# Inverse roots of a layer's RMS norms, spread over partitions by transposing their column instead of multiplying diagonal blocks by ones

## The chip, the cores and the metric

The kernel runs on one core of one Trainium2 chip. The core has five engines with queues of their own: TensorE (PE, matrix products; PEld is its weight load), VectorE (DVE), ScalarE (ACT), GpSimd (POOL) and SyncE (SP, which issues most DMA transfers). They work side by side and wait for each other by semaphores. The metric is the device time of one execution in microseconds (us), less being better.

## The reference

One decoder layer over 2048 tokens of width 1024, everything in float32: a norm, an input projection, two groups of heads side by side (a gated linear recurrence and attention with a sliding window), an output projection, a second norm, a gated feed-forward part with a short convolution, and a final norm. Cut to the norms and to where they stand:

```python
def rmsnorm(x, w, eps=EPS):
    inv = lax.rsqrt(jnp.mean(x * x, axis=-1, keepdims=True) + eps)
    return x * inv * w

u = rmsnorm(h, norm_mix_w)
proj = u @ w_in                      # 2048 x 1024 @ 1024 x 2816
...                                  # recurrence heads, attention heads -> mix
h = h + mix @ w_out
v = rmsnorm(h, norm_ffn_w)
gate = causal_depthwise_conv(v @ w_gate, conv_w, conv_b)
h = h + (silu(gate) * (v @ w_up)) @ w_down
return rmsnorm(h, final_norm_w)
```

A norm needs one number for each token: the inverse root of its mean square.

## The kernel before

**Layout.** Features lie on the 128 partitions and tokens along the free axis, eight tiles of 128 features for the width of 1024. The tokens go through in two halves of 1024 (the outermost loop). A norm's factor belongs to a token, that is to a column, and a column's factor must stand in all 128 partitions before an engine can multiply a tile by it. The kernel multiplies the matrix products first and applies the factor to their results, so a factor is needed only when a product is read back.

**Precision.** Each large product is made of three passes over split operands (high and low part); the names `XH` and `XL`, `whi` and `wlo` are these parts. Products inside the norms run on plain float32.

**A half.** The projections (names `kv`, `f`, `hq`, `q`, `g`, `pvv`, made by `unit`, line 195), the heads, the output projection (`pop`), then the feed-forward stage: eleven pairs of tiles through `pair_unit` (lines 674 to 676) for the gate and the up projection, and the down projection (`product`, lines 856 to 858), whose results `pdx` and `pdy` are added to the stream `h`. Behind the first half's down projection come the key and value projection `kv` and the first `f` of the second half.

**An inverse and its spread.** Class `Stats` holds a tile `acc` with the sums of squares, still apart for each partition. Its method `inverse` (lines 230 to 242) does three things. TensorE multiplies each block of 128 columns by a column of ones (line 236), which gives a column of totals, a token to a partition and a block to a column (`pst`). VectorE makes the inverse root of these few numbers by a bit trick and three Newton steps (`rsqrt`, lines 147 to 161, result `y`, the last step in line 160). Then VectorE writes diagonal blocks over `acc`: the identity times the column, a block of 128 columns for each (line 240). The method `spread` (lines 244 to 253) multiplies these blocks by a matrix of ones on TensorE (line 250, `pinv`, 512 columns at a time), so that each column's factor stands in every partition, and ScalarE copies the result back to `acc` (line 253).

**Where it happens.** Nine times: for the input norm `x` of each half (1024 columns, between the projections), for the feed-forward norm `h` of each half (1024 columns, inside the first `pair_unit`), for the final norm of the first half in two pieces of 512 columns (`o2` and `o`, among the `kv` projections of the second half, tile `sums`), and for the final norm of the second half in pieces of 512 (`o2`), 256 and 256 columns (`quarters`, `o`). The method `finish` (lines 944 to 948) multiplies the eight tiles of `h` by the factor and stores them. In the last two pieces it reads the factor from `pinv` itself, without a copy (`bank` given), and is bound by `issue_after(last)` to stand behind the last inverse.

**Order.** A scheduler orders the instructions of each engine by a simulated timeline of its own, within what the program's dependences and `issue_after` allow. An engine works through its own row in order.

Of the kernel before, what the change touches and what calls it, by code (L numbers as in the profile page):

```python
# [13 lines left out]
ALU = mybir.AluOpType  # L14
# [3 lines left out]
P = 128  # L18
D = 1024
# [26 lines left out]
def hymba_layer(ctx: ExitStack, tc: tile.TileContext, a: dict, out: bass.AP):  # L46
    nc = tc.nc

    def pool(name, bufs=1, space=None, stack=ctx, **kw):
        if space is not None:  # L50
            kw["space"] = space
        return stack.enter_context(tc.tile_pool(name=name, bufs=bufs, **kw))
# [12 lines left out]
    def ps(kind, name):  # L65
        return spaces[kind].tile([P, 512], F32, tag=kind, name=name)
# [9 lines left out]
    ones = cp.tile([P, P], F32, name="ones")  # L76
# [3 lines left out]
    ident = cp.tile([P, P], F32, name="ident")  # L80
# [63 lines left out]
        nc.vector.tensor_scalar(C.omlb, C.lb, -1.0, 1.0, op0=ALU.mult, op1=ALU.add)  # L144


    def rsqrt(ss, n, scale, keep=None):

        ms = sp.tile([P, n], F32, tag=f"ms{n}", name="ms")
        nc.vector.tensor_scalar(ms, ss, scale, EPS, op0=ALU.mult, op1=ALU.add)  # L150
        y = sp.tile([P, n], F32, tag=f"y{n}{keep}", name="y")
        yi = y.bitcast(I32)
        nc.vector.tensor_scalar(yi, ms.bitcast(I32), 1, None, op0=ALU.logical_shift_right)
        nc.vector.tensor_scalar(yi, yi, -1.0, float(0x5F3759DF), op0=ALU.mult, op1=ALU.add)
        nc.vector.tensor_scalar(ms, ms, -0.5, None, op0=ALU.mult)
        t = sp.tile([P, n], F32, tag=f"t{n}", name="t")
        for _ in range(3):
            nc.vector.tensor_tensor(t, y, y, op=ALU.mult)
            nc.vector.tensor_tensor(t, t, ms, op=ALU.mult)
            nc.vector.scalar_tensor_tensor(y, t, 1.5, y, op0=ALU.add, op1=ALU.mult)  # L160
        return y

    def raw4(src):
# [49 lines left out]
    class Stats:  # L213
# [16 lines left out]
        def inverse(self, keep):  # L230

            n = self.acc.shape[-1]
            nt = n // P
            st = ps("hg", "pst")
            for c in range(nt):
                nc.tensor.matmul(st[:, c:c + 1], self.acc[:, c * P:(c + 1) * P], ones[:, 0:1],
                                 start=True, stop=True)
            rs = self.rs = rsqrt(st[:, 0:nt], nt, 1.0 / D, keep)
            dg = self.acc
            return nc.vector.tensor_tensor(dg.rearrange("p (c t) -> p c t", t=P),  # L240
                                    ident.unsqueeze(1).to_broadcast([P, nt, P]),
                                    rs.unsqueeze(2).to_broadcast([P, nt, P]), op=ALU.mult)

        def spread(self, bank=None):

            n = self.acc.shape[-1]
            w = min(n, 512)
            for b in range(n // w):
                pb = ps(aux[b % 2 if bank is None else bank], "pinv")[:, 0:w]
                nc.tensor.matmul(pb, ones, self.acc[:, b * w:(b + 1) * w], start=True, stop=True)  # L250
                if bank is not None:
                    return pb
                nc.scalar.copy(self.acc[:, b * w:(b + 1) * w], pb)
# [150 lines left out]
    def hgrn(hf, h, X, invb, vs, WG, mix, p, fu=None):  # L404
# [100 lines left out]
        for c in range(TT):  # L505
# [4 lines left out]
            marks["po"] = nc.tensor.matmul(o, Q[:, cs], prev, start=False, stop=True)  # L510
            nc.scalar.activation(on[:, c], o, AF.Square, accum_out=ss[:, c:c + 1])
        rs = rsqrt(ss, TT, 1.0 / P)
        if h == HG - 1:
            mix[h] = new_x()
# [443 lines left out]
    for hf in range(NH):  # L958
        X, kv, invb, rs, f0 = nxt
        with ExitStack() as st:  # L960
            p = pool(f"mix{hf}", stack=st, reuse_waits="tile")
# [33 lines left out]
        with ExitStack() as st:  # L995
            p = pool(f"ffn{hf}", stack=st, reuse_waits="tile")
# [64 lines left out]
```

## Time and profile before

| | before |
|---|---|
| median of the runs | 2253.84 us (2253.62 to 2255.33, 3 runs) |
| span of the profiled execution (first to last instruction) | 2251.9 us |
| what lies between this span and the median | 1.9 us |
| mean granted TensorE clock | 0.990 |
| DMA, mean over the span | 113 GB/s |

The profiled execution has no device time of its own listed beside its span; the table sets the span against the median of the runs. The page gives the busy time of each engine and the chain of work that ended last; views of single lines give the duration of one instruction (least, median, most, in ns); the timeline gives start and length in us, merging neighbours of one kind (x4 is four instructions), and behind them in brackets the time its engine stood idle and what ended it. A matmul's record includes the time until its last result is out, so the records of neighbours overlap: what one costs in a stream is the distance between the ends of its neighbours, not its own length.

### The profile page before, as it was taken

The page shows a single profiled execution, that of the slowest core. Times are in us where ns is not written, and L with a number is a line of the kernel's source. Part 1 is how long each engine was busy: PE and PEld are TensorE (multiplying, and loading weights), DVE is VectorE, ACT ScalarE, POOL GpSimd, SP SyncE. Part 2 cuts the span into 40 slices and gives each one's busy share as a digit, 9 for nine tenths or more (in the row PEclk, how much of TensorE's full clock was granted, in tenths as well). Part 3 has the DMA queues.
Part 4 walks back from the last instruction along what each step waited for, and adds up shares of the span by engine and source line. Part 5 has one row for each costly group of instructions (what it writes and reads, how often), then busy time and mean ns, then how long its engine had stood idle before and what let it go on. Part 6 is the DMA issues. An engine that isn't in the chain of part 4 may idle for free.

```text
span 2251.9 us, 29785 instructions
## 1 busy us (share of the span) xinstructions
PE 2213.9 (98%) x11622; PEld 1862.1 (83%) x11622; DVE 1639.2 (73%) x2458; ACT 1024.6 (45%) x1781; POOL 7.2 (0%) x27
## 2 busy tenths in 40 slices
PE   8999999999999999999999999999999999999997
PEld 6988987778888888888889889887788888888887
DVE  6567467688888887885855665676888878887766
ACT  5345344454444444435724344435544444443353
POOL 1000000000000000000000000000000000000000
PEclk9999998999999999999999999989999999999999
DMA  4101002222323234974630101113232322359643
GB/s 151 38 29 38 29 29 75 94 85 84 118 88 122 89 122 134 360 254 148 207 122 29 38 29 29 53 51 121 67 114 97 115 92 98 107 179 390 225 136 127
DMA packets 89997, 254.19 MB, mean 113 GB/s; under 512 B 11008, under 2 KB 13184, under 8 KB 89856
## 3 DMA queue, kind: packets, MB, share of 16 engines
q1 hardware_dynamic: 87552, 251.17, 32.6%
q8 instruction: 91, 1.49, 0.3%
q10 hardware_dynamic: 2304, 1.12, 0.2%
q14 instruction: 50, 0.41, 0.1%
HBM read 195.10 MB, written 57.15 MB: 112 GB/s over the span
## 4 chain that ended last, share of the span: by engine, by line
PE 92%; DVE 4%; ACT 2%; DMA 2%; issue 1%; SPq 0%; DVEq 0%; ACTq 0%
PE X L674 7%; PE X L675 7%; PE X L676 7%; PE pop L195 6%; PE hq L195 4%; PE q L195 4%; PE f L195 4%; PE g L195 4%; PE Y L674 3%; PE Y L675 3%; PE Y L676 3%; PE pdx L856 3%; PE pdx L858 3%; PE pdx L857 3%; PE plev L454 3%; PE pdy L857 3%
## 5 line engine op out<-in xcount | busy, mean ns | idle before, releaser
L551 ACT CAST whi<-raw 128x1024 fp32r<-128x1024 f32 x88 | 92.6, 1053 | 118.6 <-PE X L675 72.8
L675 PE MATMUL X<-T,whi 128*128 128x512 f32 x352 | 137.8, 391 | 0.0
L674 PE MATMUL X<-T,whi 128*128 128x512 f32 x352 | 137.2, 390 | 0.0
L676 PE MATMUL X<-T,wlo 128*128 128x512 f32 x352 | 137.0, 389 | 0.0
L740 DVE SCALAR_TENSOR_TENSOR y<-ga,cw,y 128x1024 f32<-128x1024 f32 x88 | 112.6, 1280 | 25.4 <-ACT y L738 25.3
L176 ACT CAST whi<-raw 128x1024 fp32r<-128x1024 f32 (+2 forms) x61 | 63.0, 1036 | 123.8 <-PE q L195 59.1
L552 DVE TENSOR_TENSOR wlo<-raw,whi 128x1024 fp32r<-128x1024 f32 x88 | 107.3, 1219 | 0.0
L680 ACT COPY u<-X 128x512 f32<-128x512 f32 x88 | 51.6, 586 | 113.0 <-PE X L676 112.8
L552 DVE TENSOR_TENSOR xld<-raw,xhd 128x1024 fp32r<-128x1024 f32 x72 | 80.9, 1132 | 22.4 <-ACT xhd L551 22.0
L454 PEld LDWEIGHTS plev<-Q,K 128*128 128x128 f32 x640 | 82.8, 206 | 9.3 <-DVE K L463 4.5
L551 ACT CAST xhd<-raw 128x1024 fp32r<-128x1024 f32 x72 | 69.6, 978 | 45.9 <-DMA raw<-act0T 17.6
L454 PE MATMUL plev<-Q,K 128*128 128x64 f32 x640 | 83.5, 287 | 6.1 <-DVE K L463 6.1
L195 PE MATMUL pop<-XL,whi 128*128 128x512 f32 x256 | 84.5, 395 | 0.7 <-DVE XL L207 0.7
L195 PE MATMUL pop<-XH,wlo 128*128 128x512 f32 x256 | 84.4, 394 | 0.8 <-DVE wlo L177 0.8
L195 PE MATMUL pop<-XH,whi 128*128 128x512 f32 x256 | 84.3, 400 | 0.2
L462 DVE TENSOR_TENSOR Q<-Q,F 128x512 f32<-128x512 f32 x48 | 33.1, 690 | 67.9 <-PE plev L454 39.1
L177 DVE TENSOR_TENSOR wlo<-raw,whi 128x1024 fp32r<-128x1024 f32 (+2 forms) x61 | 73.0, 1202 | 9.3 <-ACT whi L176 9.2
L674 PEld LDWEIGHTS X<-T,whi 128*128 128x128 f32 x352 | 66.1, 188 | 14.2 <-ACT u L680 0.6
L676 PEld LDWEIGHTS X<-T,wlo 128*128 128x128 f32 x352 | 66.1, 188 | 14.2 <-issue 0.5
L675 PEld LDWEIGHTS X<-T,whi 128*128 128x128 f32 x352 | 66.1, 188 | 14.0 <-issue 0.5
L856 PE MATMUL pdx<-xhd,hid 128*128 128x512 f32 x192 | 74.5, 391 | 1.9 <-ACT hid L551 1.0
L674 PE MATMUL X<-T,Sh 128*128 128x512 f32 x176 | 70.1, 398 | 5.2 <-ACT s L680 5.2
(356 smaller groups left out, 6603.0 us busy)
## 6 DMA issues: line engine op xcount, KB each, us to landing
wr<-in_w_down SPq DMA_DIRECT2D x90, 512.0 KB, 5.5
raw<-in_w_gate SPq DMA_DIRECT2D x44, 512.0 KB, 3.6
raw<-in_w_up SPq DMA_DIRECT2D x44, 512.0 KB, 3.6
raw<-act0T SPq DMA_DIRECT2D x20, 512.0 KB, 6.5
raw<-act1T SPq DMA_DIRECT2D x20, 512.0 KB, 5.0
act0B<-y SPq DMA_DIRECT2D x33, 256.0 KB, 2.4
act1B<-y SPq DMA_DIRECT2D x33, 256.0 KB, 2.4
raw<-in_w_out SPq DMA_DIRECT2D x16, 512.0 KB, 4.0
```

Source lines behind the costliest of these rows:

```text
L177: nc.vector.tensor_tensor(lo[:, c], raw[:, c], hi[:, c].bitcast(F32), op=ALU.subtract)
L195: nc.tensor.matmul(o[b], w, x[:, bs], start=f, stop=l)
L454: mm = nc.tensor.matmul(pl[:, c * 64:(c + 1) * 64], K[:, c * P:(c + 1) * P], Qv[:, c * nbc:(c + 1) * nbc, 1], start=True, stop=True)
L551: nc.scalar.copy(h, src)
L552: (eng or nc.vector).tensor_tensor(l, src, h.bitcast(F32), op=ALU.subtract)
L674: nc.tensor.matmul(o, wh[:, ws], xh, start=i == 0 and not more, stop=False, skip_group_check=more)
L675: nc.tensor.matmul(o, wh[:, ws], xl, start=False, stop=False, skip_group_check=more)
L676: nc.tensor.matmul(o, wl[:, ws], xh, start=False, stop=i == 3, skip_group_check=more)
L740: nc.vector.scalar_tensor_tensor(y, g[:, w:w + HALF], C.cw[:, ft, w:w + 1], y, op0=ALU.mult, op1=ALU.add)
L856: nc.tensor.matmul(o, wh[:, i, c], ah[:, i, cols], start=f, stop=False, skip_group_check=more)
L857: nc.tensor.matmul(o, wh[:, i, c], al[:, i, cols], start=False, stop=False, skip_group_check=more)
L858: nc.tensor.matmul(o, wl[:, i, c], ah[:, i, cols], start=False, stop=l, skip_group_check=more)
```

## The change

The diagonal blocks go. `inverse` ends with the root; `spread` takes the column `rs[:, i:i+1]`, reads it 128 times over (a broadcast of step 0 along the free axis), and transposes that 128 x 128 view on TensorE against the identity. Row and column change places, so every partition gets the 128 factors of block `i`. Four such transposes fill what one matmul of 512 columns filled. Since `inverse` returned its last instruction (used by `issue_after`), a list `made` now keeps the last Newton steps, and the newest is returned.

```diff
+    made = []
+
     def rsqrt(ss, n, scale, keep=None):
...
         for _ in range(3):
             nc.vector.tensor_tensor(t, y, y, op=ALU.mult)
             nc.vector.tensor_tensor(t, t, ms, op=ALU.mult)
-            nc.vector.scalar_tensor_tensor(y, t, 1.5, y, op0=ALU.add, op1=ALU.mult)
+            made.append(nc.vector.scalar_tensor_tensor(y, t, 1.5, y, op0=ALU.add, op1=ALU.mult))
         return y
...
         def inverse(self, keep):
...
-            rs = self.rs = rsqrt(st[:, 0:nt], nt, 1.0 / D, keep)
-            dg = self.acc
-            return nc.vector.tensor_tensor(dg.rearrange("p (c t) -> p c t", t=P),
-                                    ident.unsqueeze(1).to_broadcast([P, nt, P]),
-                                    rs.unsqueeze(2).to_broadcast([P, nt, P]), op=ALU.mult)
+            self.rs = rsqrt(st[:, 0:nt], nt, 1.0 / D, keep)
+            return made[-1]
 
         def spread(self, bank=None):
...
                 pb = ps(aux[b % 2 if bank is None else bank], "pinv")[:, 0:w]
-                nc.tensor.matmul(pb, ones, self.acc[:, b * w:(b + 1) * w], start=True, stop=True)
+                for c in range(w // P):
+                    i = b * w // P + c
+                    nc.tensor.transpose(pb[:, c * P:(c + 1) * P], self.rs[:, i:i + 1].to_broadcast([P, P]), ident)
```

Two lines are added ahead of the class and one is lost in it, so line 236 becomes 238, line 250 becomes 251 and line 947 becomes 948. The scheduler places the spreads anew. Three places show how.

TensorE's row in the first feed-forward stage, inside the last of the seven products of the first pair (12 matmuls of `T4` into `X`), before:

```order
L676 MATMUL X_4272<-T4_4198,wlo_4008 128x512
L674 MATMUL X_4272<-T4_4198,whi_4007 128x512
L250 MATMUL pinv_4371<-invb_3505,ones_83 128x512
L250 MATMUL pinv_4374<-invb_3505,ones_83 128x512
L675 MATMUL X_4272<-T4_4199,whi_4007 128x512
```

and now (the tile `T4_4192` of before has the number 4197):

```order
L677 MATMUL X_4277<-T4_4197,wlo_4013 128x512
L675 MATMUL X_4277<-T4_4197,whi_4012 128x512
L251 MATMUL pinv_4375<-ident_87,y_4317 128x128 x4
L251 MATMUL pinv_4381<-ident_87,y_4317 128x128 x4
L676 MATMUL X_4277<-T4_4198,whi_4012 128x512
```

Two matmuls of 512 columns have become eight transposes of 128, and they stand behind the fourth of the twelve matmuls instead of the tenth: six earlier. The start of the program and the second half's feed-forward stage move by the same six.

TensorE's row at the change of halves, in the second `kv` projection; `sums` belongs to the final norm of the first half, `invb` to the input norm of the second. Before:

```order
L195 MATMUL kv1_9171<-XL_8947,whi_9165 128x512
L250 MATMUL pinv_9184<-sums_8073,ones_83 128x512
L195 MATMUL kv0_9170<-XH_8946,wlo_9166 128x512
L195 MATMUL kv1_9171<-XH_8946,wlo_9166 128x512
L195 MATMUL kv0_9170<-XH_8997,whi_9165 128x512
L195 MATMUL kv1_9171<-XH_8997,whi_9165 128x512
L250 MATMUL pinv_9215<-invb_8653,ones_83 128x512
L250 MATMUL pinv_9218<-invb_8653,ones_83 128x512
L195 MATMUL kv0_9170<-XL_8998,whi_9165 128x512
```

and now (`y_9105` is the root of the final norm, `y_9154` that of the input norm):

```order
L197 MATMUL kv0_9180<-XL_8803,whi_9175 128x512
L251 MATMUL pinv_9194<-ident_87,y_9105 128x128 x4
L197 MATMUL kv1_9181<-XL_8803,whi_9175 128x512
L197 MATMUL kv0_9180<-XH_8802,wlo_9176 128x512
L197 MATMUL kv1_9181<-XH_8802,wlo_9176 128x512
L197 MATMUL kv0_9180<-XH_8846,whi_9175 128x512
L197 MATMUL kv1_9181<-XH_8846,whi_9175 128x512
L197 MATMUL kv0_9180<-XL_8847,whi_9175 128x512
L197 MATMUL kv1_9181<-XL_8847,whi_9175 128x512
L251 MATMUL pinv_9228<-ident_87,y_9154 128x128 x4
L251 MATMUL pinv_9234<-ident_87,y_9154 128x128 x4
L197 MATMUL kv0_9180<-XH_8846,wlo_9176 128x512
```

Both spreads stand nearer to the sums that they come from: 26 `kv` matmuls now lie between the last sum of the input norm (line 236, now 238) and the first of these transposes, and 33 before the second group. On VectorE the eight multiplies of line 947 for the other 512 columns come earlier with their spread, and one split of a weight (line 177) now stands near the end of the Newton steps and no longer ahead of most of them.

VectorE's row at the end of the program, before:

```order
L158 TENSOR_TENSOR t<-y 128x2
L159 TENSOR_TENSOR t<-t,ms 128x2
L160 SCALAR_TENSOR_TENSOR y<-t,y 128x2
L240 TENSOR_TENSOR invb<-ident,y 128x256
L947 TENSOR_TENSOR h_16260<-h_16260,pinv 128x256
```

and now:

```order
L160 TENSOR_TENSOR t<-y 128x2
L161 TENSOR_TENSOR t<-t,ms 128x2
L162 SCALAR_TENSOR_TENSOR y<-t,y 128x2
L948 TENSOR_TENSOR h_16284<-h_16284,pinv 128x256
L948 TENSOR_TENSOR h_16286<-h_16286,pinv 128x256
```

The diagonal is gone, and the sixteen multiplies of `finish` follow the last Newton step directly.

## The prediction

> **What bounds the kernel now.** I read the page first: the span, the busy time of each engine, and the engine shares of the chain that ended last.
>
> ```profile
> span 2251.9 us, 29785 instructions
> PE 2213.9 (98%) x11622; PEld 1862.1 (83%) x11622; DVE 1639.2 (73%) x2458; ACT 1024.6 (45%) x1781; POOL 7.2 (0%) x27
> PE 92%; DVE 4%; ACT 2%; DMA 2%; issue 1%; SPq 0%; DVEq 0%; ACTq 0%
> ```
>
> TensorE is busy 98% of the span and carries 92% of the chain, so its time in the stream is the currency; VectorE work counts only where TensorE waits for it. Next I read the list of who TensorE waited for; these are the rows near the change.
>
> ```profile
> PE kv L195 <- ACT XH L209: 6.6, 1, 6.6
> PE plev L454 <- DVE K L463: 6.1, 5, 2.7
> PE X L674 <- ACT s L680: 5.2, 2, 2.6
> PE pinv L250 <- DVE invb L240: 2.3, 1, 2.3
> ```
>
> The columns are total, number of waits and longest. TensorE waits for a diagonal (line 240) only once, 2.3 us, and that is at the very end. At the other eight inverses it comes to line 250 with the diagonal long made. So the change has two separate prices: TensorE's own time in the stream, and VectorE's time in the tail.
>
> **What is removed.** These are the instructions of lines 250 and 240, with their duration as least/median/most in ns.
>
> ```profile
> L250 PE MATMUL pinv<-invb,ones x22: 379/592/794, 43.0 to 2243.1; 128*128 128x512 f32 x18, 128*128 128x256 f32 x4
> L250 PE MATMUL pinv<-sums,ones x4: 590/590/591, 1128.8 to 1145.0; 128*128 128x512 f32 x4
> L240 DVE TENSOR_TENSOR invb<-ident,y x7: 425/1220/1226, 36.8 to 2242.0; 128x1024 f32<-128x1024 f32 x4, 128x256 f32<-128x256 f32 x2, 128x512 f32<-128x512 f32 x1
> L240 DVE TENSOR_TENSOR sums<-ident,y x2: 685/689/693, 1124.4 to 1138.8; 128x512 f32<-128x512 f32 x2
> ```
>
> A float32 matmul is two records: the program has 13 spreading matmuls, the trace 26. Eleven are 512 wide (18 and 4 records), eight of them in the four inverses of 1024 columns and three in those of 512; two are 256 wide. The durations overlap, so the price in the stream is read from the ends of the neighbours, first around a pair of spreads, then around a single one.
>
> ```profile
> 42.31 0.61 PE L195 MATMUL f<-XH,whi 128*128 128x512 f32 x2
> 42.76 0.39 PE L195 MATMUL f<-XL,whi 128*128 128x512 f32 x1
> 42.99 1.88 PE L250 MATMUL pinv<-invb,ones 128*128 128x512 f32 x4
> 44.31 0.80 PE L195 MATMUL f<-XL,whi 128*128 128x512 f32 x1
> ...
> 1128.54 0.39 PE L195 MATMUL kv<-XH,wlo 128*128 128x512 f32 x1
> 1128.77 1.02 PE L250 MATMUL pinv<-sums,ones 128*128 128x512 f32 x2
> 1129.23 0.79 PE L195 MATMUL kv<-XH,whi 128*128 128x512 f32 x1
> ```
>
> Columns are start and length. The first row holds two stream matmuls and the third starts 0.45 later, so each takes 0.225. The one before the pair ends at 42.76 + 0.39 = 43.15, the one behind it at 44.31 + 0.80 = 45.11: 1.96 apart, of which 0.225 is its own. A pair of spreads costs **1.73 us**. In the same way the single one costs 1130.02 - 1128.93 - 0.225 = **0.865 us**.
>
> **What is added on TensorE.** Four transposes of 128 columns per 512. The trace has the same operation, float32 against the same identity, on other data; here, under a row of VectorE that the next paragraph needs, are its two rows and one instance of four in a stream.
>
> ```profile
> L227 DVE TENSOR_TENSOR invb<-invb,x x14: 1194/1221/1228, 15.8 to 1118.7; 128x1024 f32<-128x1024 f32 x14
> ...
> L307 PEld LDWEIGHTS pv<-ident,vT x16: 138/140/142, 50.9 to 1165.9; 128*128 128x128 f32 x16
> L307 PE MATMUL pv<-ident,vT x16: 270/272/273, 51.1 to 1166.0; 128*128 128x128 f32 x16
> ...
> 50.88 0.39 PE L195 MATMUL hq<-XH,wlo 128*128 128x512 f32 x1
> 51.11 0.60 PE L307 MATMUL pv<-ident,vT 128*128 128x128 f32 x4
> 51.46 0.48 PE L195 MATMUL hq<-XH,whi 128*128 128x512 f32 x1
> ```
>
> Sixteen records for sixteen transposes: one pass each, not two. Four of them cost 51.94 - 51.27 - 0.225 = **0.445 us**, 0.111 each. What no row shows is a weight load whose 128 columns are one column read again and again (step 0). From below, a transpose might be as cheap as a quarter of a stream matmul, 0.225 / 4 = 0.056; from above, load and pass might run one behind the other, 0.140 + 0.272 = 0.41. I take 0.111: form, width and identity are those of line 307, and the nearest step-0 reading costs nothing. That is line 240 on VectorE, which reads both operands by repetition and takes 1220 ns for 1024 columns, as line 227 does (1221 ns) without any.
>
> So a 1024-column spread falls from 1.73 to 0.89, saving 0.84, and a 512-column one from 0.865 to 0.445, saving 0.42. All seven lie in the stream, the two of 256 columns in the tail: 4 x 0.84 + 3 x 0.42 = **4.6 us**.
>
> The Trainium skill, TensorE: Matmul & The Clock Gate, section Part 4: PE-mode transpose, speaks against the change: it gives about 275 ns for a transpose in a kernel's context, and says that a transpose does not count as activity for the clock. By 275 ns each, the 44 transposes in the stream would take an estimated 12.1 us and the gain would turn into a loss. The duration agrees (272 ns), but the trace's four take 0.60 us together, so they overlap.
>
> **What is moved.** The scheduler puts the spreads 6 matmuls earlier at the start and in each feed-forward stage, 11 earlier for the first 512-column inverse between the halves; for the other two there, 26 and 33 matmuls now lie between the last sum (line 236) and the transposes. The question is whether the root is made by then.
>
> ```profile
> 36.50 0.17 DVE L160 SCALAR_TENSOR_TENSOR y<-t,y 128x8 f32<-128x8 f32 x1
> ...
> 502.51 0.16 DVE L160 SCALAR_TENSOR_TENSOR y<-t,y 128x8 f32<-128x8 f32 x1
> ...
> 508.34 1.88 PE L250 MATMUL pinv<-invb,ones 128*128 128x512 f32 x4
> ...
> 1122.55 0.16 DVE L160 SCALAR_TENSOR_TENSOR y<-t,y 128x4 f32<-128x4 f32 x1
> 1122.62 0.68 DVE L842 TENSOR_TENSOR h<-h,pdx 128x512 f32<-128x512 f32 x1
> ...
> 1133.75 1.84 PE L236 MATMUL pst<-ones,invb 128*128 128x1 f32 x16
> ...
> 1138.61 0.28 DVE L160 SCALAR_TENSOR_TENSOR y<-t,y 128x4 f32<-128x4 f32 x2
> ```
>
> At 0.225 a matmul, the spreads would come at 41.6 for a root of 36.7, at 507.0 for 502.7, and at 1126.3 for 1122.7. Between the halves the roots end 3.3 us behind the last sum (1135.6 to 1138.9), and the transposes stand 5.9 and 7.4 us behind it. No wait is added; the least cover is 2.6 us. In the other queues a store of an activation (SyncE, once in each half) and a weight cast and two bias steps (ScalarE) change places with their neighbours, in stretches where TensorE waits for nothing. On VectorE nine diagonals go, about 8 us, but eight of them were beside TensorE's stream: nothing for those.
>
> **The tail.** Here TensorE has nothing left, and VectorE's row is the path.
>
> ```profile
> 2241.81 0.16 DVE L160 SCALAR_TENSOR_TENSOR y<-t,y 128x2 f32<-128x2 f32 x1
> 2242.01 0.42 DVE L240 TENSOR_TENSOR invb<-ident,y 128x256 f32<-128x256 f32 x1
> 2242.35 5.38 DVE L947 TENSOR_TENSOR h<-h,pinv 128x256 f32<-128x256 f32 x16
> ...
> 2242.49 1.22 PE L250 MATMUL pinv<-invb,ones 128*128 128x256 f32 x2 [2.34 <-DVE invb L240]
> ...
> 2245.49 4.01 SPq L948 DMA_DIRECT2D out<-h  x8
> ```
>
> Sixteen multiplies follow the last diagonal, 0.336 apart; the first eight use the first quarter's spread, done long before, and the other eight start at 2245.04, over a microsecond after the last spread. So the spread itself hides and the diagonal does not. Without it the first multiply follows the root's last step, on which it does not depend, 0.07 later (as 1122.62 follows 1122.55): 2241.88 and not 2242.35, **0.47 us** saved; 0.34, the diagonal's own slot, if it has to wait for that step. The stores move with it.
>
> **Sum.** 4.6 + 0.5 = 5.1 us. The profiled execution lasted 2251.9 by its span; the median of the runs is 2253.84, 1.9 more, which lies around the span and should stay. The forecast is 2253.84 - 5.1 = **2248.7 us**. A measurement tells about 0.2% from no change, 4.5 us here: the forecast is just beyond it.
>
> **Rivals.**
> Part of the gain is lost at the next wait for something that TensorE does not pace. For it: the plev waits (6.1 us) come after the start and after the change of halves. Against it: what they wait for hangs itself on the spreads. If the gain of those four spreads goes (0.84 + 0.42 + 0.42 + 0.84), 2.6 us stay: 2251.2.
>
> The clock shifts. Both feed-forward stages begin with a wait of 2.6 us (X L674 above) and then run slowly.
>
> ```profile
> 484.00:487.50 3.50, 0.94 (x5) 0.43 (x3) 3.50 (x7) 3.41 (x7) 0.00 (x0) 1.00 0.40 152
> 487.50:491.50 4.00, 3.94 (x10) 3.15 (x11) 4.00 (x7) 1.67 (x4) 0.00 (x0) 0.57 0.40 131
> ```
>
> The column behind POOL's is the granted clock: 0.57 for 4 us costs 1.7 us. Earlier work may move one such stretch out: 2247.0; a new one would give 2250.4.
>
> Slower: the step-0 weight load can't be pulled ahead of the pass before it, so each transpose takes 0.140 + 0.272 = 0.41. Then 44 x 0.30 = 13.2 us come back and the kernel takes 2261.9. It breaks even at 0.227 a transpose and is measurably slower from 0.33. Line 307's 0.60 for four speaks against it, but with ordinary columns.
>
> Transposes in line at their own 0.272, loads hidden: 44 x 0.161 = 7.1 lost, 2255.8. This is what the skill's section, named above, would give; the four in 0.60 us speak against it.
>
> The change doesn't do what it says, each transpose being two passes as a matmul is: 44 x 0.111 = 4.9 lost, 2253.6. The sixteen records for sixteen transposes speak against it.
>
> **How the numbers follow.** Forecast (2247.7 to 2249.9) 0.55; partly lost 0.22; a better clock 0.11; serial loads 0.05; in line 0.05; two passes 0.02. About four fifths of the forecast's own cases lie below 2249.3, which with the better clock makes faster 0.55. Slower is the serial loads alone, 0.05; the rest, 0.40, is within 0.2%. The range takes in the better clock and the partly lost gain with one clock stretch of doubt: 2246.5 to 2252.0, without the dearer transposes.
>
> **What would show it.** Right: four transposes of line 251 in about 0.6 us, the neighbours' ends 0.89 us further apart than one matmul around eight; no wait of TensorE for y outside the tail; the first multiply of the tail 0.1 to 0.2 after the last root step's start. Wrong: weight loads of line 251 well over 140 ns, a start-to-start of transposes over 0.2 us, or a clock below 0.9 behind them.

## The result, and the profile after

| | before | changed |
|---|---|---|
| median, first comparison (18 runs each) | 2253.70 us (2249.73 to 2259.78) | 2250.22 us (2245.34 to 2252.49) |
| ratio to before | 1 | 0.9983 (0.9976 to 0.9990): -3.8 us (-5.4 to -2.3) |
| second comparison (21 and 11 runs) | 2253.73 us | 2249.62 us; ratio 0.9979 (0.9970 to 0.9988): -4.7 us (-6.8 to -2.7) |
| span of the profiled execution | 2251.9 us | 2250.0 us, and 2246.5 us in a second one |

The changed kernel is faster, by 3.8 and 4.7 us where 5.1 were forecast; both intervals hold the forecast and leave out zero. In what follows, a difference to before in us is the ratio less one, times the median of before in the same comparison.

The page of the changed kernel has the span, the busy time of each engine and the engine shares of the chain of waits:

```profile
span 2250.0 us, 29825 instructions
PE 2210.9 (98%) x11644; PEld 1864.7 (83%) x11644; DVE 1633.1 (73%) x2449; ACT 1023.8 (46%) x1781; POOL 6.0 (0%) x27
PE 93%; DVE 4%; DMA 1%; ACT 1%; issue 0%; SPq 0%; DVEq 0%; ACTq 0%
```

TensorE has 22 records more (48 transposes for 26 matmul passes) and is busy 3.0 us less; VectorE loses nine instructions and 6.1 us. The list of who TensorE waits for (total, times, longest):

```profile
PE kv L197 <- ACT XH L211: 8.9, 2, 7.2
PE X L675 <- ACT s L681: 5.8, 2, 3.2
PE plev L455 <- DVE K L464: 5.8, 4, 2.7
PE pinv L251 <- DVE y L162: 2.1, 1, 2.1
```

The transposes wait for the root (`y`) once, in the tail, where they waited for the diagonal before. None of the moved spreads has a wait of its own. The first row was 6.6 us before; both of its waits end before 14 us, ahead of the first spread. The groups of line 251 (least, median and most ns, first and last start):

```profile
L251 PEld LDWEIGHTS pinv<-ident,y x48: 133/137/227, 43.9 to 2240.6; 128*128 128x128 f32 x48
L251 PE MATMUL pinv<-ident,y x48: 270/272/473, 44.2 to 2240.8; 128*128 128x128 f32 x48
```

There are 48 records for 48 transposes, one pass each, and a weight load that reads one column 128 times takes 137 ns, no more than the 140 ns of an ordinary tile in line 307. The price in the stream is again the distance between the neighbours' ends on the timeline:

```profile
43.93 0.39 PE L197 MATMUL f<-XL,whi 128*128 128x512 f32 x1
44.16 1.03 PE L251 MATMUL pinv<-ident,y 128*128 128x128 f32 x8
44.95 0.48 PE L197 MATMUL f<-XL,whi 128*128 128x512 f32 x1
...
1140.58 0.39 PE L197 MATMUL kv<-XL,whi 128*128 128x512 f32 x1
1140.80 0.60 PE L251 MATMUL pinv<-ident,y 128*128 128x128 f32 x4
1141.16 0.48 PE L197 MATMUL kv<-XL,whi 128*128 128x512 f32 x1
```

Eight cost 45.43 - 44.32 - 0.225 = 0.885 us, four 1141.64 - 1140.97 - 0.225 = 0.445, where the matmuls cost 1.73 and 0.865. In the tail, VectorE's timeline has the last root step and the multiplies of `finish`:

```profile
2240.34 0.16 DVE L162 SCALAR_TENSOR_TENSOR y<-t,y 128x2 f32<-128x2 f32 x1
2240.42 5.38 DVE L948 TENSOR_TENSOR h<-h,pinv 128x256 f32<-128x256 f32 x16
```

The multiplies start 0.08 behind the step, 0.54 before.

The profiled pair differs by only 1.9 us. The first of the sums of line 236 (238 now) stands just ahead of the first spread, the last of them in the tail; their rows of before, and of the changed kernel, show where the rest is:

```profile
L236 PE MATMUL pst<-ones,invb x80: 164/250/271, 32.3 to 2239.4; 128*128 128x1 f32 x80
```

```profile
L238 PE MATMUL pst<-ones,invb x80: 164/250/353, 34.8 to 2237.9; 128*128 128x1 f32 x80
```

The changed kernel was 2.5 us late at the first of them, ahead of anything that the change touches. Between first and last it took 2203.1 us instead of 2207.1, 4.0 less. Of the 2.5 us, 1.7 are a stretch at half clock that this execution had at the start, the row by windows of the changed kernel being

```profile
14.00:17.40 3.40, 3.40 (x10) 2.69 (x9) 2.90 (x4) 3.40 (x4) 0.00 (x0) 0.53 0.93 270
```

where before has a granted clock (third column from the end) of 1.00. Longer waits for the first `kv` products, 9.1 us in all against 8.1, make most of the rest. Neither is a part of the change: the second profiled execution of the changed kernel has its first sum at 32.6.

### The profile page after: what moved, and what is told of

Read it like the earlier page. It is cut to its first block, busy times and chain, and to the rows that moved or that the text cites. A ratio compares the mean times of both kernels' runs of the same rounds, so it can differ in the third digit from the quotient of the medians.

```text
span 2250.0 us, 29825 instructions
## 1 busy us (share of the span) xinstructions
PE 2210.9 (98%) x11644; PEld 1864.7 (83%) x11644; DVE 1633.1 (73%) x2449; ACT 1023.8 (46%) x1781; POOL 6.0 (0%) x27
## 3 DMA queue, kind: packets, MB, share of 16 engines
q1 hardware_dynamic: 87552, 251.17, 32.7%
## 4 chain that ended last, share of the span: by engine, by line
PE 93%; DVE 4%; DMA 1%; ACT 1%; issue 0%; SPq 0%; DVEq 0%; ACTq 0%
PE X L675 7%; PE X L676 7%; PE X L677 7%; PE pop L197 6%; PE hq L197 4%; PE q L197 4%; PE f L197 4%; PE g L197 4%; PE pdx L857 4%; PE Y L675 4%; PE pdx L858 4%; PE pdx L859 4%; PE Y L676 3%; PE Y L677 3%; PE plev L455 3%; PE pdy L858 3%
```

## The experiments

My theory after the result: the gain in the stream is the price of TensorE's own instructions, 44 transposes at 0.109 to 0.111 us in place of eleven matmuls at 0.865, and the tail is VectorE's diagonal. The first rival: the gain comes of VectorE, which loses nine diagonals and gets its other work done sooner. The second: an instruction put into the stream is partly absorbed by waits, so that neighbours' distances don't carry to the end.

**Two passes.** The transposes as plain float32 matmuls against the identity:

```diff
-nc.tensor.transpose(pb[:, c * P:(c + 1) * P], self.rs[:, i:i + 1].to_broadcast([P, P]), ident)
+nc.tensor.matmul(pb[:, c * P:(c + 1) * P], self.rs[:, i:i + 1].to_broadcast([P, P]), ident, start=True, stop=True)
```

> The 48 transposes are issued as ordinary float32 matmuls with the same step-0 weights and the same identity; the diagonals stay away. Stream theory (the gain is TensorE's own time): 44 more passes of 0.111 us are 4.9 us, so 5.1 - 4.9 = 0.2 us below before, and the neighbours of eight end about 2.0 us apart (1.78 + 0.225). VectorE theory (the gain comes from the nine diagonals that went): as the changed kernel, 3.5 us below before. Absorbed theory (a third of TensorE's stream time is lost in later waits): about 0.5 us below before.

Ratio 1.0013 (1.0004 to 1.0023), +2.9 us (0.9 to 5.2). All three expectations missed. Yet the stream of this kernel has the price that the first theory gave:

```profile
504.39 0.39 PE L676 MATMUL X<-T,whi 128*128 128x512 f32 x1
504.62 1.95 PE L251 MATMUL pinv<-ident,y 128*128 128x128 f32 x16
506.32 0.48 PE L677 MATMUL X<-T,whi 128*128 128x512 f32 x1
```

Sixteen passes cost 506.80 - 504.78 - 0.225 = 1.795 us, against 1.73 for the ones matmuls. Some 3 us were unexplained.

**Five times the work.** The spreads of the stream repeated five times, in the changed kernel and in the one of before:

```diff
-for c in range(w // P):
+for c in [c for _ in range(5 if bank is None else 1) for c in range(w // P)]:
```

```diff
+for _ in range(5 if bank is None else 1):
-nc.tensor.matmul(pb, ones, self.acc[:, b * w:(b + 1) * w], start=True, stop=True)
+    nc.tensor.matmul(pb, ones, self.acc[:, b * w:(b + 1) * w], start=True, stop=True)
```

> The changed kernel with each spread in the stream transposed five times into the same place; the two of 256 columns once. Stream theory: 4 x 44 x 0.111 = 19.5 us more than the changed kernel, 14.4 us above before. Absorbed theory: two thirds of it, about 13 more, 9.5 us above before. A step-0 load that can't be pulled ahead: 4 x 44 x 0.41 = 72 us more.

> The kernel before with each ones matmul in the stream issued five times. Stream theory: 4 x (4 x 1.73 + 3 x 0.865) = 38 us above before, and 38.1 - 14.4 = 23.7 us (five times 4.6 and the tail's 0.5) above the changed kernel with five transposes. Absorbed theory: about 25 us above before, 16 above the other.

Transposes: ratio 1.0080 (1.0065 to 1.0095), +18.0 us (14.6 to 21.4). Matmuls: 1.0158 (1.0145 to 1.0171), +35.6 us (32.7 to 38.5). Absorption (+9.5 and +25) is out for both, and so are serial loads. The matmuls came out at the stream's price; the transposes a little above it, with the expected 14.4 just below the interval, and the two kernels lie 17.2 us apart by the medians and not 23.7. Yet on the timeline forty transposes have their price exactly, as have, in the second fence, the twenty passes of the matmuls:

```profile
509.42 0.39 PE L675 MATMUL X<-T,whi 128*128 128x512 f32 x1
509.64 4.53 PE L251 MATMUL pinv<-ident,y 128*128 128x128 f32 x40
513.93 0.48 PE L676 MATMUL X<-T,whi 128*128 128x512 f32 x1
```

```profile
513.94 0.39 PE L675 MATMUL X<-T,whi 128*128 128x512 f32 x1
514.17 8.74 PE L251 MATMUL pinv<-invb,ones 128*128 128x512 f32 x20
522.35 0.80 PE L676 MATMUL X<-T,whi 128*128 128x512 f32 x1
```

(514.41 - 509.81 - 0.225) / 40 = 0.109 us a transpose; (523.15 - 514.33 - 0.225) / 10 = 0.86 us a matmul. Again about 3.5 us were missing (18.0 - 14.4).

**VectorE's diagonals put back.** Scratch diagonals, written and never read, behind the inverses of the stream (44 of 256 columns, in bf16), and in the second kernel behind each of the two last inverses (8). The lines stand at the end of `inverse`; the range is the only difference:

```diff
+for k in range(nt if n > 256 else 0):      # in the tail: 8 if n == 256 else 0
+    dg = sp.tile([P, 256], BF16, tag="dg", name="dg", bufs=1)
+    made.append(nc.vector.tensor_tensor(dg..., ident..., self.rs[:, 2 * k % nt:2 * k % nt + 2]..., op=ALU.mult))
 return made[-1]
```

> The changed kernel with 44 multiplies of 256 columns added on VectorE behind the seven inverses in the stream (identity times the root into a scratch tile that nobody reads), about 15 us of VectorE, twice what the change took away there. Stream theory: as the changed kernel, within 0.5 us. VectorE theory: the gain is lost twice over, about 3.5 us above before.

> The changed kernel again, beside the other two. Stream theory: 5.1 us below before. Absorbed theory: 2.6 to 3.5 below.

> The changed kernel with eight multiplies of 256 columns behind each of the two last inverses (VectorE, scratch tile), ahead of the sixteen last multiplies. If the tail is VectorE's path: 0.47 + 7 x 0.34 = 2.9 us above the changed kernel, all of it behind the last inverse; the eight behind the first quarter's inverse hide. If the tail is bound by the stores or by the last spread: less than 1 us.

In the stream: ratio 0.9983 (0.9974 to 0.9992), the changed kernel's own. The changed kernel once more: 0.9979. In the tail: 1.0000 (0.9992 to 1.0009), 3.5 us above the changed kernel by the medians (2253.14 and 2249.62). So VectorE's diagonals have no cost beside the stream that the intervals (2 us either way) show, and their full length in the tail, as VectorE's timeline of the last kernel has it (the window ends at 2246, within the sixteen multiplies):

```profile
2238.28 0.16 DVE L163 SCALAR_TENSOR_TENSOR y<-t,y 128x2 f32<-128x2 f32 x1
2238.48 3.64 DVE L244 TENSOR_TENSOR dg<-ident,y 128x256 bf16<-128x256 f32 x8
2242.03 4.05 DVE L954 TENSOR_TENSOR h<-h,pinv 128x256 f32<-128x256 f32 x12
```

The first multiply comes 3.75 us behind the step, not 0.08: 3.7 more where 2.9 were expected, since the eight scratch diagonals stand 0.46 apart and not 0.34. The rival of VectorE falls: it asked for 3.5 us above before, and the kernel with the diagonals in the stream is 3.8 below. That they are entirely free isn't shown. In the profiled execution of that kernel TensorE has a wait that the changed kernel's list lacks:

```profile
PE ppt L386 <- DVE m L365: 3.2, 1, 3.2
```

The same execution has 24 us of half clock where the two of the changed kernel have 34 to 38, which saves some 5 us and can hide that wait. Taken at the same mean clock, the runs of this kernel lie 2.5 to 4.6 us below before, so a cost of one or two us beside the stream stays possible.

**Another order of two products.** The waits of 2.6 us at the first gate pair, with the half clock behind them, had nothing to do with the change, but stood out in the profile. The kernel issues the product Y ahead of Z there:

```diff
+        Y = ps("hg", "Y")
+        if then:
+            prod(Y, "S1", "T1")
+            s5 = out(Y, "s5")
+        first = bool(then)
         Z = ps("at", "Z")
...
-        Y = ps("hg", "Y")
-        prod(Y, "S1", "T1")
-        s5 = out(Y, "s5")
+        if not first:
+            prod(Y, "S1", "T1")
+            s5 = out(Y, "s5")
```

> The changed kernel with one order changed: in the first gate pair of each half the product Y (S1 with T1) is issued ahead of Z and of the second product into X, for which TensorE waits 2.6 us and behind which its clock is halved for 3.4 us or more. If the wait was for work that Y can cover and the clock follows from it: 3 to 8 us below the changed kernel. If ScalarE's and VectorE's queues are the bound there, the wait moves behind Y: the same within 1 us.

Ratio 0.9953 (0.9940 to 0.9965), -10.6 us (-13.5 to -7.9), 5.9 below the changed kernel by the medians (2243.75), within the 3 to 8 expected: it beats both. Its list of waits shows what went:

```profile
PE X L675 <- ACT s L681: 0.4, 1, 0.4
```

**The missing 3 us.** Setting the instruction rows of these kernels side by side showed what I had not controlled. The scheduler's simulated timeline decides the order, and in the two-pass kernel, the one with five times the transposes and the one with Y first it had put the products of the *later* feed-forward pairs into another order. Counted over the matmuls of the traces, by the names of their tiles without buffer numbers, some 3,100 to 3,900 lines of TensorE's row are lost or new against the changed kernel, nearly all of them in X, Y and Z, where before and the changed kernel differ in 128, and the five times repeated matmuls and before in 170. In the old order some products into X follow each other, 24 matmuls on end; in the other one nearly all alternate with Y and Z. So these kernels differ in two things. Four more keep them apart. The first has ten times the transposes and the second two passes in the spreads outside the feed-forward norm only, which leaves the order alone; the third doubles only those of that norm, which flips it; the fourth has Y first on the kernel of before, in the old order.

```diff
-def spread(self, bank=None):
+def spread(self, bank=None, k=10):          # third kernel: k=1
-    for c in range(w // P):
+    for c in [c for _ in range(k if bank is None else 1) for c in range(w // P)]:
...
-then = {..., "S4": lambda: (hs.spread(), flush())} if pr == 0 else {}
+then = {..., "S4": lambda: (hs.spread(k=1), flush())} if pr == 0 else {}      # third kernel: k=2
```

> Every spread in the stream but the two of the feed-forward norm is transposed ten times over: 28 transposes more, nine times, 252 in all. The later products of the feed-forward pairs keep the order that they have in the changed kernel. If a transpose costs 0.109 us in the stream, as neighbours' ends show, and the kernels in which all spreads were repeated or run in two passes were slower by some 3 us for the other order of their feed-forward products, then 252 x 0.109 = 27.5 us above the changed kernel, 22.8 above before (ratio 1.0101). If the order is of no account and a transpose truly costs what the five times repeated kernel gives (22.7 / 176 = 0.129), 32.5 above the changed kernel and 27.8 above before (1.0123).

> The transposes of all spreads but those of the feed-forward norm are issued as float32 matmuls against the identity, two passes each; the later feed-forward products keep the order of the changed kernel. Each of these 28 in the stream then costs 0.224 and not 0.109: 3.2 us above the changed kernel, 1.5 below before (0.9993). If the kernel with two passes everywhere was slower than this price for a reason of the passes themselves and not of its order, 28/44 of its excess of 3.1 us come on top: 0.5 above before (1.0002).

> Only the two spreads of the feed-forward norm are transposed twice: 16 transposes more. The scheduler answers by putting the products of the later feed-forward pairs into the other order, that of the two-pass kernel. If that order costs about 3.3 us (2.9 + 0.2 from the two-pass kernel, 3.5 from the five times repeated one), this kernel is 16 x 0.109 + 3.3 = 5.0 us above the changed kernel and about the time of before (+0.4 us, ratio 1.0002). If the order costs nothing and a transpose is 0.109 to 0.129, it is 1.7 to 2.1 above the changed kernel and 2.8 below before (0.9988).

> The kernel of before, with the product Y issued ahead of Z in the first gate pair of each half, as in the kernel that beat both. The later products keep the order of before. If the gain of that kernel came of the two waits of 2.6 us at the first gate pair (X L675 for the ScalarE copy s) and of the stretches at half clock behind them, one or two of 3.41 us and 1.7 us each in each half, it is 2 x 2.6 + 2 x 1.7 = 8.6 us below before (0.9962), and the two gains add up. If it came of the other order of the later products, which that kernel has and this one has not, it is within 2 us of before (0.9991 to 1.0).

| kernel | expected by my account (the order costs; Y first gains by the waits) | by the rival | measured |
|---|---|---|---|
| ten times, old order | +22.8 | +27.8 | +21.4 (18.2 to 24.6) |
| two passes, old order | -1.5 | +0.5 | -1.6 (-3.6 to 0.5) |
| feed-forward norm twice, other order | +0.4 | -2.8 | +1.8 (-0.5 to 3.8) |
| Y first on before, old order | -8.6 | -2 to 0 (gain from the order) | -7.2 (-9.9 to -4.5) |

The first and the third exclude the account without the order; the second leans the same way, and its interval just reaches the other value. The third also has more work in the spreads of the feed-forward norm, as the two-pass kernel and the one with five times the transposes have, so that this place might be to blame. The kernel with five times the matmuls answers that: it has 14 us more work in those spreads alone (16 matmuls at 0.865), keeps the old order, and came out at its price. What the order costs is one difference of the third to the changed kernel: 1.8 + 4.7 - 1.75 for its sixteen transposes, about 5 by this comparison (4 with the 3.8 of the first) and 3 by the other two kernels, with some 3 us of doubt. Part of it is seen in the waits at the start of the down projection. This is the row of the third kernel, and behind it that of the second, in the old order:

```profile
PE pdx L857 <- ACT hid L552: 3.4, 2, 2.7
```

```profile
PE pdx L860 <- ACT hid L555: 1.0, 2, 0.5
```

All eight kernels of the old order (before and changed among them) have 1.0 in this row; the four of the other order have 3.0 to 3.9, 2.0 to 2.9 us more. In three of them a further part is in the clock. This is the row by windows of the third kernel, in which the wait of 2.7 us ends at 918.4:

```profile
917.60:921.60 4.00, 3.20 (x8) 2.57 (x9) 4.00 (x6) 1.79 (x2) 0.00 (x0) 0.57 0.82 279
```

A granted clock of 0.57 for 4 us is 1.7 us more. The kernel with five times the transposes and the one with Y first on the changed kernel have the same 0.57 behind waits of 2.1 and 2.3 us in this place; the two-pass kernel, with 1.3 us there, has 1.00, and so have all eight of the old order. Wait and clock come to 3.7 to 4.6 us in three of them and to 2.0 in the two-pass kernel, read from one execution each, which in the third kernel was its slowest.

Y first is a gain by itself, 7.2 us without the change and 5.9 with it, where the other order comes along; that this order costs 3 us there too can't be told from two numbers that are each uncertain by some 3 us. With the wait its half clock goes too. The row by windows of the kernel with Y first on before is

```profile
484.00:492.00 8.00, 8.00 (x45) 6.73 (x44) 7.99 (x13) 4.73 (x9) 0.00 (x0) 1.00 0.29 101
```

TensorE is busy through all 8 us at a granted clock of 1.00, where before stood idle for 2.6 us and then ran at 0.57.

## Why the prediction was right, point by point

**TensorE bounds, VectorE only in the tail.** Right: 44 scratch multiplies beside the stream left the gain as it was (3.8 us), eight in the tail cost their length.

**The price of a transpose.** Right. 0.111 us was taken from line 307; eight cost 0.885 us (0.84 saved), four 0.445 (0.42 saved), and 80 in one go give 0.109, below. The bound from above, 0.41 for a load that can't be pulled ahead, would have cost 0.30 more each, 66 us in the kernel with 220 transposes in the stream and 89 in that with 296.

**The sum in the stream, 4.6 us.** The profiled pair took 4.0 less between the sums' first and last record, the second execution of the changed kernel 2201.8 and so 5.3 less. Between these records the stretches at half clock add up to the same 34.1 us in all three executions, so the clock is no part of these differences. The intervals of the two comparisons (2.3 to 5.4, 2.7 to 6.8) both hold 5.1. The first rival (2.6 us left of all) lies inside the first and just outside the second; the two profiled executions speak against it.

The recorded clock of each run says more. In the second comparison, runs of the same mean granted clock differ on average by 4.5 us at 0.989, 4.3 at 0.990, 4.6 at 0.991 and 4.4 at 0.992 (4, 5, 1 and 1 runs of the changed kernel beside 4, 8, 8 and 1 of before). So the gain isn't a better clock, and by this comparison about 4.4 of the 5.1 us came: the sum was somewhat too high, and the first rival too low. Read in the same way, the kernel with five times the matmuls is 37.7 and 38.0 above before (38 expected) and the one with ten times the transposes 22.2 to 22.6 (22.8 expected). Where the missing 0.7 us went isn't shown. By its median the first comparison (2250.22) lies just outside the forecast's own band of 2247.7 to 2249.9, the second (2249.62) inside; and the 3.8 us of the first stay below the 4.5 that the prediction wanted for telling a gain from none, though its interval leaves out zero.

**No wait added.** Right: no row for `y` outside the tail.

**The tail.** 0.47 forecast. From the end of the last down-projection matmul to the end it takes 13.89 us (2236.11 to 2250.0), before 14.32: 0.43 saved, and 0.47 in the second execution (2232.65 to 2246.5): the forecast's term and not the 0.34 of the diagonal's slot alone. The first multiply starts 0.08 behind the last root step, a little less than the 0.1 to 0.2 named as a sign.

**The rivals.** Serial loads, transposes in line at 0.272, and two passes are excluded for this kernel by the neighbours' ends and the 48 records. The Trainium skill, TensorE: Matmul & The Clock Gate, section Part 4: PE-mode transpose, has the duration of a single one right (272 ns here in float32, against about 275 in one kernel, given beside a bf16 figure), but here the distance in a stream, 0.109 to 0.111 us, is the price, and not that duration. The shifting clock is real and belongs to the execution: the changed kernel's 18 runs have 2250.9 us on average at a mean granted clock of 0.989 (9 runs) and 2248.6 at 0.991 (2 runs).

**What I had not seen.** The prediction asked what the reordering moves around the spreads and priced it at nothing, which held, since the change alters few rows. It did not ask whether the scheduler could answer a change of a microsecond or two with another order of the whole stage behind it. The experiments met that three times, and a fourth provoked it; the forecast was right partly because the change didn't, and nothing in the prediction says why it shouldn't have.

## What to carry to other kernels

A column can be spread over the partitions by transposing a step-0 view of it, at 0.11 us for 128 columns in TensorE's stream against 0.22 for float32 matmuls with ones, without the diagonal; price such an edit by the distance of neighbours' ends, not by durations. Where a scheduler decides the order, compare the instruction rows of every experiment with its parent's before reading its time: an edit that costs 1.7 us by itself can flip a stage that costs 3 more. A wait of 2.6 us on the bounding engine can cost more than itself, as the clock behind it halves; here moving one product over it gave more than the change did.

## What the runs showed of the hardware

Stretches at half clock come in multiples of 3.41 us (3.41, 6.83, 13.65 and 17.07 in before and the changed kernel), and the wait of 2.6 us at the first gate pair is followed by a short one in before and a long one in the changed kernel. The rows by windows of the changed kernel around that wait are

```profile
484.00:488.20 4.20, 1.58 (x7) 0.98 (x7) 4.20 (x6) 4.11 (x8) 0.00 (x0) 1.00 0.44 151
488.20:495.40 7.20, 7.20 (x24) 5.96 (x23) 5.66 (x10) 1.94 (x4) 0.00 (x0) 0.53 0.15 59
```

7.2 us near 0.5, where before had 4 at 0.57. It is a matter of the execution: in the second one of the changed kernel the same 7.2 us have a granted clock of 0.76. Each such step is worth 1.7 us, nearly half of what the change gains, and the runs of one kernel lie a few such steps apart. The Trainium skill, TensorE: Matmul & The Clock Gate, section Part 1: The HAM clock gate (the "warmup" mystery), gives 3413 ns for the window in which activity is judged; the steps agree.

Transposes alone keep a full clock up. The timeline of the kernel with ten times the spreads has 80 on end, and its row by windows, in the second fence, shows the clock:

```profile
41.91 0.39 PE L197 MATMUL f<-XL,whi 128*128 128x512 f32 x1
42.14 8.89 PE L251 MATMUL pinv<-ident,y 128*128 128x128 f32 x80
50.79 0.48 PE L197 MATMUL f<-XL,whi 128*128 128x512 f32 x1
```

```profile
42.30:51.20 8.90, 8.90 (x83) 8.86 (x81) 1.29 (x2) 2.05 (x4) 0.00 (x0) 1.00 0.01 2
51.20:60.00 8.80, 8.80 (x42) 7.25 (x41) 6.35 (x8) 5.98 (x8) 0.00 (x0) 1.00 0.05 13
```

(51.27 - 42.30 - 0.225) / 80 = 0.109 us each, and the granted clock is 1.00 through them and behind them. Whether transposes can raise a lowered clock wasn't tried. The statement of the Trainium skill, TensorE: Matmul & The Clock Gate, section Part 4: PE-mode transpose, that a transpose doesn't count as activity in the same way, isn't borne out here as far as keeping the clock goes.
